# Two feed-forward stages: the up products over an operand whose high and low parts lie side by side

## The chip, the cores and the metric

The kernel runs on one core of one Trainium2 chip. The metric is device time in microseconds of one execution, as the median of several. One execution was also taken with the hardware profiler, and all rows below come from that one.

## The reference, cut to what matters

The program is a transformer layer for 256 tokens of 1024 features, all in float32: two attention kinds and a mixture of experts in a first block, then a second block of axial attention, cross attention, feed-forward 0, a mixer, cross attention, feed-forward 1 and a final norm. The change is about the two feed-forward stages:

```python
x = x + conv_gated_ffn(rmsnorm_2(x, ffn_norm[i]), ffn_w_up[i], ffn_conv_w[i],
                       ffn_conv_b[i], ffn_w_down[i])

# conv_gated_ffn: up to 2 x 2816 features, a convolution of three taps
# along the tokens with a bias, then
    return (jax.nn.silu(gate) * val) @ w_down
```

So each token's 1024 features are divided by their root mean square and multiplied by a gain, widened to 5632 features, mixed with the neighbour tokens' values, gated, and brought back to 1024 features.

## The kernel before, in words

**Numbers in two parts.** A float32 value is kept as a high part and a low part. A product of two such values is three matmuls, low by high, high by high and high by low, all added in PSUM (`mm3`, L363 to L366). The weights pass through in blocks of 128x1024: SP's queue loads a block (`w`), ACT copies its high part at L275 (`whi`, four buffers), DVE subtracts at L284 (`wlo`, three buffers), and PE uses the pair. `get` hands out block n and emits the high part of block n+3 and the low part of block n+2, so the `wlo` of block n+2 goes to the buffer that block n-1 leaves, and waits in DVE's order until PE is done with block n-1.

**A feed-forward stage** (`ffn`, L1751) has 22 steps j. In a step, `up(j)` (L1767) takes two blocks: for each, eight chunks of 128 rows, each with three matmuls of 256 columns (`two_blocks`, 48 matmuls, into one PSUM bank, tags "s" and "tp" by turns). Then `act_steps(j)` follows on DVE and ACT: `u` = sums times 1/rms (DVE, L1777), `y` = middle tap and bias (ACT, L1782, two of them), the two other taps (DVE, four of L1786/L1787), the gate (ACT, L1789), their product (DVE, L1791), its high part `gTh` (ACT, L1793) and its low part `gTl` (DVE, L1795). `down(j-3)` (L1802) is 12 matmuls of 512 columns with `gTh` and `gTl` as the stationary side, into four PSUM banks that collect over the whole stage. Its fifth matmul is the first that reads `gTl`.

The operand of `up` is x times gain, not yet divided by the rms: the stage begins while the last residual sums are still being added. The root comes behind it: `columns` three blocks in, `rows` (L467) four blocks in, and `nrep` (L473) then holds 1/rms along the free axis for L1777. Four `turn`s (L1809, at j = 4, 8, 12, 16) transpose the residual for the end of the stage.

**What sets the order.** Each engine runs its instructions in the order in which the program emits them. `act_steps` is a generator. After each weight block, `tick` lets the generators in `side` advance by turns until a credit is spent; `finish` advances them until the named one has ended, and `down_all(j)` calls it for step j before its matmuls. The blocks of a stage follow as: up(0) 0, 1; up(1) 2, 3; up(2) 4, 5; up(3) 6, 7; down(0) 8; up(4) 9, 10; down(1) 11; up(5) 12, 13; down(2) 14; and so on, three a step.

Of the kernel before, what the change touches and what calls it, by code (L numbers as in the profile page):

```python
# [32 lines left out]
T = 256  # L33
NT = 2
# [29 lines left out]
def _constants():  # L64
# [23 lines left out]
    # mean over the window of each group, minus the token itself  # L88
# [62 lines left out]
def body(tc, a, out, dbg=None):  # L151
# [44 lines left out]
    # keys and values of the memory, to be worked on wherever TensorE would wait  # L196
# [39 lines left out]
    with top:  # L236
# [8 lines left out]
        ps = pool(top, "ps", space=PS)  # L245
        NB = {"mm": 3, "s": 3, "tp": 2}

        def bank(tag="mm", dt=FT):
            return ps.tile([128, 512], dt, name=tag, tag=tag, bufs=NB[tag])

# [16 lines left out]
        def cuts(n, f):  # L267
            # the very first block in halves, to begin earlier
            return [slice(0, f // 2), slice(f // 2, f)] if n == 0 else [slice(0, f)]
# [89 lines left out]
        def split_to(hi, lo, src):  # L359
            S.activation(hi, src, AF.Copy)  # L360
            V.tensor_sub(lo, src, hi.bitcast(FT))

# [13 lines left out]
        # (the tables of ScalarE come in while the first loads run)  # L376
# [19 lines left out]
        class Norm:  # L396
# [21 lines left out]
            def square(self, p):  # L418
# [25 lines left out]
            def squares(self):  # L444
                """their squares over the head width, for the norms of the heads"""
# [15 lines left out]
            def spread(self):  # L461
                """1/rms of the tokens, along the free axis of every partition."""
# [15 lines left out]
        def h_pair():  # L478
            return (hp.tile([128, KC, T], FR, name="hTh", tag="hTh"), hp.tile([128, KC, T], FR, name="hTl", tag="hTl"))
# [11 lines left out]
        def two_blocks(aT, blocks, o, lead=False):  # L491
            """two blocks of 128 features; as a lead side by side, for an operand whose last chunks are still to come"""
# [16 lines left out]
        class Feat:  # L509
            """features on partitions: two blocks of 128 a bank"""  # L510
# [24 lines left out]
        class Tok:  # L535
            """tokens on partitions: 512 features, a bank for each half of the tokens"""
# [32 lines left out]
        def head_roots(stk, sq, H, nm, t):  # L569
            """1/rms of the heads, without that of the tokens"""  # L570
# [6 lines left out]
        def flip_heads(dst, src, t, two=False):  # L577
            """dst[feature, pair, token] from src[token, head, 64]; `two` doubles each head into a pair"""
# [98 lines left out]
            # what the scores of each head are scaled by: 1/rms, and 1/8  # L677
# [169 lines left out]
                # a block for each head of a pair  # L847
# [3 lines left out]
            # -- stages of causal attention for the two heads of a pair --  # L851
# [54 lines left out]
            # -- projections and the compressed keys and values --  # L906
# [64 lines left out]
            # -- the heads, pair by pair, with projections in between --  # L971
# [81 lines left out]
            # -- merge: g0 * up_a(ya) + g1 * up_b(yb), with g = (1 + tanh) / 2 --  # L1053
# [36 lines left out]
        # high and low parts of the keys side by side  # L1090
# [37 lines left out]
        # -- routing, a few operations at a time --  # L1128
# [17 lines left out]
        def route():  # L1146
# [12 lines left out]
            def keys(q):  # L1159
                """keys of the kept pairs, of four heads"""  # L1160
                hs, ks = ts(q, 4), ts(q, 64)
                for t in range(NT):
# [11 lines left out]
                    for e in range(2):  # L1174
# [3 lines left out]
                        if q == 0:  # L1178
                            # (whole numbers: 1 where they are equal, 0 elsewhere)
# [36 lines left out]
            # gates: softmax over the kept ones  # L1216
# [16 lines left out]
            # the gates (in 0..1, times GATE) as a sum of two float16 parts  # L1233
# [40 lines left out]
        # -- gates in place: one-hot products, two tokens side by side --  # L1274
# [22 lines left out]
        def one_hot(half, j):  # L1297
            # the wide scratch of the norms is free here
# [53 lines left out]
        # -- second products; their sum goes to the residual --  # L1352
# [643 lines left out]
```

## Time and profile before

| | us |
|---|---|
| three runs | 1767.97, 1765.30, 1765.14 |
| median | 1765.3 |
| span of the profiled execution | 1767.7 |
| PE busy in that span | 1734.9 (98%) |
| DVE busy | 1375.0 (78%) |
| ACT busy | 940.7 (53%) |

The profile's span is that of one execution of its own, 2.4 us above the median of the timed ones. Busy time of PE counts the whole of pipelined matmuls; the distance from one matmul's start to the next one's is what tells how fast they go. Feed-forward 0 lies from about 1256 to 1447 us of the span, feed-forward 1 from about 1569 us to the end.

### The profile page before, as it was taken

The numbers are of one execution on the slowest core, as the hardware profiler recorded it, in microseconds if no ns is written. First come the engines' busy times: TensorE is split into PE (matmuls) and PEld (weight loads), VectorE is DVE, ScalarE is ACT, GpSimd is POOL, SyncE is SP. The second block draws the span as 40 slices with busy tenths as digits, with TensorE's granted clock in tenths as the row PEclk, the third lists the DMA queues.
The fourth block names the chain that finished last, engine by engine and source line by source line (L and its number), as shares of the span: only waits on it lengthen the run. The fifth ranks groups of instructions, "written<-read, shape, count | busy, mean of one in ns | idle before, by whom it ended". The sixth has DMA issues, their size and how long they took to land. (4 is left out here: it accounts for less than half of the span.)

```text
span 1767.7 us, 32012 instructions
## 1 busy us (share of the span) xinstructions
PE 1734.9 (98%) x12638; PEld 1579.8 (89%) x12638; DVE 1375.0 (78%) x2435; ACT 940.7 (53%) x1396; POOL 174.7 (10%) x127
## 2 busy tenths in 40 slices
PE   8999999999999999999999999999999999999998
PEld 7877999999999998888888887799999999899997
DVE  7788879999878776999666657875788876678777
ACT  5556555455544344444454554655566566556555
POOL 1210020155200000000010003010200002020000
PEclk9999999999999999999999999999999999999999
DMA  6633454555544545555655654243556554455553
GB/s 210 202 121 100 148 166 161 195 168 168 193 164 167 166 161 186 164 173 167 214 190 191 194 170 153 84 156 121 192 181 202 179 174 160 132 183 189 179 181 129
DMA packets 83094, 297.66 MB, mean 168 GB/s; under 512 B 9264, under 2 KB 10304, under 8 KB 82816
## 3 DMA queue, kind: packets, MB, share of 16 engines
q1 hardware_dynamic: 81072, 291.41, 49.9%
q0 software_dynamic: 608, 2.62, 0.4%
q8 instruction: 99, 1.62, 0.4%
q10 hardware_dynamic: 1264, 1.59, 0.3%
q14 instruction: 51, 0.42, 0.1%
HBM read 294.54 MB, written 1.05 MB: 167 GB/s over the span
## 5 line engine op out<-in xcount | busy, mean ns | idle before, releaser
L275 ACT ACTIVATE whi<-w 128x1024 fp32r<-128x1024 f32 (+1 forms) x554 | 583.1, 1055 | 445.8 <-PE s L1366 151.8
L284 DVE TENSOR_TENSOR wlo<-w,whi 128x1024 fp32r<-128x1024 f32 (+1 forms) x554 | 700.2, 1269 | 148.2 <-issue 67.4
L364 PE MATMUL s<-hTl,whi 128*128 128x256 f32 x1024 | 292.5, 286 | 0.0
L366 PE MATMUL s<-hTh,wlo 128*128 128x256 f32 x1024 | 290.2, 283 | 1.2 <-DVE wlo L284 1.1
L365 PE MATMUL s<-hTh,whi 128*128 128x256 f32 x1024 | 289.6, 283 | 0.0
L366 PEld LDWEIGHTS s<-hTh,wlo 128*128 128x128 f32 x1024 | 196.3, 192 | 2.1 <-DVE wlo L284 2.0
L364 PEld LDWEIGHTS s<-hTl,whi 128*128 128x128 f32 x1024 | 196.3, 192 | 0.1
L365 PEld LDWEIGHTS s<-hTh,whi 128*128 128x128 f32 x1024 | 196.4, 192 | 0.0
L364 PE MATMUL mm<-hTl,whi 128*128 128x256 f32 (+1 forms) x488 | 140.1, 287 | 0.0
L366 PE MATMUL mm<-hTh,wlo 128*128 128x256 f32 (+1 forms) x488 | 138.8, 285 | 0.8 <-DVE wlo L284 0.7
L365 PE MATMUL mm<-hTh,whi 128*128 128x256 f32 (+1 forms) x488 | 138.7, 284 | 0.0
L1366 PE MATMUL mm<-wlo,hTh 128*128 128x512 f32 x381 | 131.3, 398 | 0.0
L1366 PE MATMUL mm<-whi,hTh 128*128 128x512 f32 x381 | 128.4, 390 | 0.0
L1366 PE MATMUL mm<-whi,hTl 128*128 128x512 f32 x381 | 128.1, 390 | 0.0
L364 PE MATMUL tp<-xTl,whi 128*128 128x256 f32 x352 | 99.7, 283 | 0.0
L366 PE MATMUL s<-xTh,wlo 128*128 128x256 f32 x352 | 99.6, 283 | 0.0
L366 PE MATMUL tp<-xTh,wlo 128*128 128x256 f32 x352 | 99.6, 283 | 0.0
L365 PE MATMUL s<-xTh,whi 128*128 128x256 f32 x352 | 99.5, 283 | 0.0
L365 PE MATMUL tp<-xTh,whi 128*128 128x256 f32 x352 | 99.4, 282 | 0.0
L364 PE MATMUL s<-xTl,whi 128*128 128x256 f32 x352 | 98.9, 281 | 0.0
L366 PEld LDWEIGHTS mm<-hTh,wlo 128*128 128x128 f32 (+1 forms) x488 | 93.6, 192 | 1.3 <-DVE wlo L284 1.2
L364 PEld LDWEIGHTS mm<-hTl,whi 128*128 128x128 f32 (+1 forms) x488 | 93.4, 191 | 0.7 <-issue 0.4
(451 smaller groups left out, 3914.4 us busy)
## 6 DMA issues: line engine op xcount, KB each, us to landing
w<-in_p_u_dram SPq DMA_DIRECT2D x128, 512.0 KB, 3.3
w<-in_p_v_dram SPq DMA_DIRECT2D x128, 512.0 KB, 3.3
w<-in_f_up_dram SPq DMA_DIRECT2D x88, 512.0 KB, 3.2
w<-in_f_down_dram SPq DMA_DIRECT2D x44, 512.0 KB, 3.8
w<-in_w_tok_dram SPq DMA_DIRECT2D x19, 512.0 KB, 3.4
w<-in_w_mg_dram SPq DMA_DIRECT2D x16, 512.0 KB, 3.5
w<-in_p_wq_dram SPq DMA_DIRECT2D x16, 512.0 KB, 3.3
w<-in_x_k_dram SPq DMA_DIRECT2D x16, 512.0 KB, 3.4
```

Source lines behind the costliest of these rows:

```text
L275: S.activation(hi[:, c], w[:, c], AF.Copy)
L284: V.tensor_sub(lo[:, c], w[:, c], hi[:, c].bitcast(FT))
L364: mm(o, l[0], r[1], start=start, stop=False, **kw)
L365: mm(o, l[0], r[0], start=False, stop=False, **kw)
L366: mm(o, l[1], r[0], start=False, stop=stop, **kw)
L1366: mm(acc[2 * h + t], l[k], w[m][:, ts(h, 512)], start=c == 0 and k == 0 and m == 1, stop=c == 127 and k == 1)
```

## The change

Up to the sixth step a stage runs as before, over x times gain. From the seventh on (`J0 = 6`) it runs over an operand that is already divided by the rms, `hN`.

- `h_pair` is now one tile with the high and the low part of each chunk next to each other (this holds for every user of `h_pair`).
- `normed_steps`, a generator among the others, makes `hN` once 1/rms is there: four DVE multiplications of 128x512, eight ACT copies and eight DVE subtractions of 128x256.
- `mm_side` takes the place of `mm3` in the steps from j = 6: for each chunk, the high weights run once over 512 columns (high and low part of `hN`), the low weights over 256. The two halves of the result stand in two halves of a bank.
- `act_steps` from j = 6: ACT copies the second half, DVE adds the first to it. This replaces the multiplication by 1/rms.
- PSUM: the banks are closed and opened anew for each stage. `up` gets two tiles of two banks each, the sums of `down` four banks that `columns`, `rows` and the turns use first. All four turns are now at j = 1 and 2. Before a tile is taken again, `wait_freed` advances the generators until its sums have been read.

```diff
         def h_pair():
-            return (hp.tile([128, KC, T], FR, name="hTh", tag="hTh"), hp.tile([128, KC, T], FR, name="hTl", tag="hTl"))
+            return Pair(hp.tile([128, KC, 2, T], FR, name="hT", tag="hT"))
...
+        def mm_side(o, w, aT):
+
+            for kc in range(KC):
+                mm(o, w[0][:, ts(kc)], merge(aT.t[:, kc]), start=kc == 0, stop=kc == KC - 1, skip_group_check=True)
+                mm(o[:, 0:T], w[1][:, ts(kc)], aT[0][:, kc], start=False, stop=kc == KC - 1, skip_group_check=True)
...
+                def normed_steps():
+
+                    for p in range(4):
+                        tag = ("nsq", "nacc")[p % 2]
+                        x = pairs(st_.tile([128, 512], FT, name=tag, tag=tag, bufs=1))
+                        V.tensor_tensor(x, xT[:, 2 * p:2 * p + 2], nm_.rep2(), op=OP.mult)
+                        yield
+                        for k in range(2):
+                            c = 2 * p + k
+                            g = gcol[:, gi, c:c + 1]
+                            S.activation(hN[0][:, c], x[:, k], AF.Copy, scale=g)
+                            V.scalar_tensor_tensor(hN[1][:, c], x[:, k], g, hN[0][:, c].bitcast(FT), op0=OP.mult, op1=OP.subtract)
+                        yield
+
+                J0 = 6
+                after(3, first_columns)
+                after(4, first_rows)
...
+                        o = Banks.pool.tile([128, 1024], FT, name="up", tag="up", bufs=2)
+                    if j < J0:
+                        if j % 2 == 0:
+                            first_up[0] = o
+                        o = first_up[0][:, ts(j % 2, 512)]
+                        two_blocks(hT, blocks, o, j == 0)
+                        tick()
+                        return o
+                    finish(normed)
+                    for e in range(2):
+                        mm_side(o[:, ts(e, 512)], get(*blocks[e]), hN)
+                        tick()
                     return o
...
-                    V.tensor_tensor(u, pairs(o), nm_.rep2(), op=OP.mult)
+                    if j < J0:
+                        V.tensor_tensor(u, pairs(o), nm_.rep2(), op=OP.mult)
+                    else:
+                        ov = o.rearrange("p (e s t) -> p e s t", e=2, s=2)
+                        S.activation(u, ov[:, :, 1], AF.Copy)
+                        yield
+                        V.tensor_tensor(u, ov[:, :, 0], u, op=OP.add)
+                    freed.add(j)
...
                 for j in range(NJ):
                     o = up(j)
+                    if j == 1 or j == 2:
+                        turn(2 * j - 2)
+                        turn(2 * j - 1)
+                    if j == 3:
+                        acc_[:] = [side_bank() for _ in range(4)]
                     acts.append(spawn(act_steps(j, o)))
```

On PE, a piece of one `up` in the steps from the seventh on. Before, three matmuls a chunk, with `xTl` and `xTh` as the low and high part of the operand:

```order
L364 MATMUL s<-xTl,whi 128x256
L365 MATMUL s<-xTh,whi 128x256
L366 MATMUL s<-xTh,wlo 128x256
L364 MATMUL s<-xTl,whi 128x256
L365 MATMUL s<-xTh,whi 128x256
L366 MATMUL s<-xTh,wlo 128x256
```

and now, with the end of the `down` before it, two a chunk:

```order
L1895 MATMUL acc<-wlo,gTh 128x512 x2
L1895 MATMUL acc<-whi,gTh 128x512 x2
L1895 MATMUL acc<-whi,gTl 128x512 x2
L388 MATMUL up<-hT,whi 128x512
L389 MATMUL up<-hT,wlo 128x256
L388 MATMUL up<-hT,whi 128x512
L389 MATMUL up<-hT,wlo 128x256
```

The columns of a chunk are the same, 768, in two matmuls and two weight loads where there were three of each.

On DVE, feed-forward 0, from the low weights of block 5 on. Before (y_14486/7 are the two halves of step 0, y_14557/8 of step 1), up to `gTl` of step 0:

```order
L1777 TENSOR_TENSOR u<-tp,nrep 128x512
L1786 SCALAR_TENSOR_TENSOR y_14486<-u,cw,y_14486 128x255
L1787 SCALAR_TENSOR_TENSOR y_14486<-u,cw,y_14486 128x255
L1786 SCALAR_TENSOR_TENSOR y_14487<-u,cw,y_14487 128x255
L1787 SCALAR_TENSOR_TENSOR y_14487<-u,cw,y_14487 128x255
L284 TENSOR_TENSOR wlo<-w,whi 128x1024 x2
L1786 SCALAR_TENSOR_TENSOR y_14557<-u,cw,y_14557 128x255
L1787 SCALAR_TENSOR_TENSOR y_14557<-u,cw,y_14557 128x255
L1786 SCALAR_TENSOR_TENSOR y_14558<-u,cw,y_14558 128x255
L1787 SCALAR_TENSOR_TENSOR y_14558<-u,cw,y_14558 128x255
L1791 TENSOR_TENSOR y_14486<-y_14486,y_14487 128x256
L284 TENSOR_TENSOR wlo<-w,whi 128x1024
```

Now (y_14529/30 are step 0), the piece around the product of step 0 and its `gTl`, with the low weights of blocks 9 and 10:

```order
L298 TENSOR_TENSOR wlo<-w,whi 128x1024
L1817 TENSOR_TENSOR nsq<-xT,nrep 128x512
L1884 TENSOR_TENSOR y_14529<-y_14529,y_14530 128x256
L1823 SCALAR_TENSOR_TENSOR hT<-nsq,first,hT 128x256 x2
L1888 TENSOR_TENSOR gTl<-y_14529,gTh 128x256
L298 TENSOR_TENSOR wlo<-w,whi 128x1024
L1434 SCALAR_TENSOR_TENSOR meml<-memT,first,memh 128x256
L1864 TENSOR_TENSOR u<-up,nrep 128x512
```

and the rows behind it, where y_14716/7 are the halves of step 1 and y_14761/2 those of step 2, and the two low weights are those of blocks 11 and 12:

```order
L1817 TENSOR_TENSOR nacc<-xT,nrep 128x512
L298 TENSOR_TENSOR wlo<-w,whi 128x1024
L1823 SCALAR_TENSOR_TENSOR hT<-nacc,first,hT 128x256 x2
L298 TENSOR_TENSOR wlo<-w,whi 128x1024
L1879 SCALAR_TENSOR_TENSOR y_14716<-u,cw,y_14716 128x255
L1880 SCALAR_TENSOR_TENSOR y_14716<-u,cw,y_14716 128x255
L1879 SCALAR_TENSOR_TENSOR y_14717<-u,cw,y_14717 128x255
L1880 SCALAR_TENSOR_TENSOR y_14717<-u,cw,y_14717 128x255
L1864 TENSOR_TENSOR u<-up,nrep 128x512
L1884 TENSOR_TENSOR y_14716<-y_14716,y_14717 128x256
```

What moved: the taps of step 1 stood ahead of step 0's product and of the low weights of block 9; now they stand behind the low weights of block 12, and the rows that make `hN` (L1817, L1823) are in between. Feed-forward 1 has the same order there.

## Rows read from the trace of the kernel before

**Rows 1.** The page: span, and each engine's busy time, share and instructions.

```profile
span 1767.7 us, 32012 instructions
PE 1734.9 (98%) x12638; PEld 1579.8 (89%) x12638; DVE 1375.0 (78%) x2435; ACT 940.7 (53%) x1396; POOL 174.7 (10%) x127
```

**Rows 2.** Steps of feed-forward 0 as one stretch; PEclk is the granted clock.

```profile
core 0: us, PE busy (x) PEld busy (x) DVE busy (x) ACT busy (x) POOL busy (x), PEclk, DMA share, GB/s
1282.00:1440.00 158.00, 158.00 (x1107) 147.59 (x1106) 131.02 (x202) 98.55 (x148) 1.07 (x2) 1.00 0.56 186
```

**Rows 3.** PE timeline, one step of feed-forward 0: start, duration, instruction.

```profile
1333.89 0.63 PE L1802 MATMUL mm<-wlo,gTh 128*128 128x512 f32 x2
...
1336.46 0.39 PE L1802 MATMUL s<-whi,gTl 128*128 128x512 f32 x1
1336.69 0.28 PE L364 MATMUL s<-xTl,whi 128*128 128x256 f32 x1
...
1342.45 0.64 PE L1802 MATMUL mm<-wlo,gTh 128*128 128x512 f32 x2
...
1350.89 0.29 PE L366 MATMUL tp<-xTh,wlo 128*128 128x256 f32 x1
1351.02 0.64 PE L1802 MATMUL mm<-wlo,gTh 128*128 128x512 f32 x2
```

**Rows 4.** PE timeline, the experts' second products: first and last of a stretch.

```profile
860.00 0.62 PE L1366 MATMUL mm<-wlo,hTh 128*128 128x512 f32 x2
...
870.88 0.62 PE L1366 MATMUL mm<-wlo,hTh 128*128 128x512 f32 x2
```

**Rows 5.** Timelines of PE and DVE where the feed-forward stages begin.

```profile
1569.17 0.28 PE L364 MATMUL s<-xTl,whi 128*128 128x256 f32 x1
...
1569.37 0.69 DVE L560 TENSOR_TENSOR xT<-xT,mm 128x512 f32<-128x512 f32 x1 [0.24 <-PE mm L366]
...
1269.61 0.68 PE L467 MATMUL tp<-ndg,ones 128*128 128x128 f32 x4 [1.05 <-DVE ndg L458]
```

**Rows 6.** Durations of the normalised operand made elsewhere (tile hn): min/median/max ns.

```profile
L1123 ACT ACTIVATE hTh<-hn,first x8: 493/496/499, 286.7 to 289.5; 128x256 fp32r<-128x256 f32 x8
L1124 DVE SCALAR_TENSOR_TENSOR hTl<-hn,first,hTh x8: 465/476/477, 288.1 to 290.8; 128x256 fp32r<-128x256 f32 x8
```

**Rows 7.** A stretch of feed-forward 1's first steps, columns as in rows 2.

```profile
1582.00:1594.00 12.00, 12.00 (x98) 11.86 (x98) 11.25 (x18) 9.22 (x15) 0.00 (x0) 1.00 0.49 165
```

**Rows 8.** DVE timeline of feed-forward 1, steps 0 and 1.

```profile
1584.24 0.68 DVE L1777 TENSOR_TENSOR u<-tp,nrep 128x512 f32<-128x512 f32 x1
1584.84 0.47 DVE L1786 SCALAR_TENSOR_TENSOR y<-u,cw,y 128x255 f32<-128x255 f32 x1
...
1586.66 2.35 DVE L284 TENSOR_TENSOR wlo<-w,whi 128x1024 fp32r<-128x1024 f32 x2
1588.93 0.48 DVE L1786 SCALAR_TENSOR_TENSOR y<-u,cw,y 128x255 f32<-128x255 f32 x1
...
1590.76 0.42 DVE L1791 TENSOR_TENSOR y<-y,y 128x256 f32<-128x256 f32 x1
1591.10 1.22 DVE L284 TENSOR_TENSOR wlo<-w,whi 128x1024 fp32r<-128x1024 f32 x1
```

**Rows 9.** ACT timeline of feed-forward 1: the y pair, and gTh of step 0.

```profile
1583.22 1.09 ACT L1782 ACTIVATE y<-u,cw 128x256 f32<-128x256 f32 x2 [0.76 <-DVE u L1777]
...
1591.21 0.42 ACT L1793 ACTIVATE gTh<-y 128x256 fp32r<-128x256 f32 x1 [1.33 <-DVE y L1791]
```

**Rows 10.** A long PE wait and the clock behind it, then a short one.

```profile
1068.30 1.02 PE L434 MATMUL tp<-ones,nacc 128*128 128x2 f32 x4 [2.90 <-POOL nacc L428]
...
1068.00:1072.00 4.00, 3.70 (x11) 3.12 (x12) 1.63 (x4) 1.06 (x1) 0.96 (x2) 0.50 0.35 131
1072.00:1076.00 4.00, 4.00 (x14) 3.15 (x13) 1.35 (x5) 2.07 (x5) 0.00 (x0) 0.66 0.40 131
1268.00:1272.00 4.00, 2.95 (x25) 2.77 (x24) 2.12 (x4) 0.91 (x3) 2.12 (x3) 1.00 0.65 219
```

More of the change, by code (lines that the diff above doesn't have):

```diff
@@ L244, in body, with open, close @@
         hp = pool(top, "h")
-        ps = pool(top, "ps", space=PS)
         NB = {"mm": 3, "s": 3, "tp": 2}
+        class Banks:
+            stack = pool = None
+            @classmethod
+            def open(cls, name):
+                cls.stack = ExitStack()
+                cls.pool = pool(cls.stack, name, space=PS)
+            @classmethod
+            def close(cls):
+                cls.stack.close()
+        Banks.open("ps")
         def bank(tag="mm", dt=FT):
-            return ps.tile([128, 512], dt, name=tag, tag=tag, bufs=NB[tag])
+            return Banks.pool.tile([128, 512], dt, name=tag, tag=tag, bufs=NB[tag])
         class Stream:
@@ L361, in split_to, with __new__ @@
             V.tensor_sub(lo, src, hi.bitcast(FT))
+        class Pair(tuple):
+            def __new__(cls, t):
+                self = tuple.__new__(cls, (t[:, :, 0], t[:, :, 1]))
+                self.t = t
+                return self
+        def mm_side(o, w, aT):
+            for kc in range(KC):
+                mm(o, w[0][:, ts(kc)], merge(aT.t[:, kc]), start=kc == 0, stop=kc == KC - 1, skip_group_check=True)
+                mm(o[:, 0:T], w[1][:, ts(kc)], aT[0][:, kc], start=False, stop=kc == KC - 1, skip_group_check=True)
         def mm3(o, l, r, start, stop, **kw):
@@ L1358, in w_split @@
             h, cc = divmod(c, HALF)
-            split_to(*(merge(x) for x in cut(wT, ALL, slice(c % 8, c % 8 + 2))), merge(A[h][:, cc:cc + 2]))
+            split_to(*cut(wT, ALL, slice(c % 8, c % 8 + 2)), A[h][:, cc:cc + 2])
         def v_mm(c, w, t, hs=(0, 1)):
@@ L1715, in fin @@
                             mm3(o[:, ts(c, T)], cut(xv[i], ALL, k, ts(cc)), cut(pT, ALL, k), k == 0, k == 1)
-                    split_to(merge(oT[0][:, 2 * h:2 * h + 2]), merge(oT[1][:, 2 * h:2 * h + 2]), o)
+                    split_to(oT[0][:, 2 * h:2 * h + 2], oT[1][:, 2 * h:2 * h + 2], pairs(o))
                 ss = [sco(0), sco(1)]
@@ L1758, in ffn @@
                 nc.sync.dma_start(cw, a[f"f_conv{i}"])
-                acc_ = [bank("mm") for _ in range(3)] + [bank("s")]
-                acc[:] = acc_
                 nm_ = nm
-                after(3, nm_.columns)
-                after(4, nm_.rows)
+                gi = nm_.gi
                 gTs = {}
-                tags = ["s", "tp"]
-                def up(j):
-                    o = bank(tags[j % 2])
-                    two_blocks(hT, [(f"f_up{i}", e * NJ + j) for e in range(2)], o, j == 0)
-                    tick()
+                acc_ = []
@@ new lines, in ffn, with side_bank, first_columns, first_rows @@
+                hN = h_pair()
+                def side_bank():
+                    return Banks.pool.tile([128, 512], FT, name="acc", tag="acc", bufs=4)
+                def first_columns():
+                    o = side_bank()
+                    for t in range(NT):
+                        mm(o[:, 2 * t:2 * t + 2], nm_.acc[:, ts(t)], ones[:, 0:2], start=True, stop=True)
+                    nm_.root(o)
+                def first_rows():
+                    nm_.diagonal()
+                    o = side_bank()
+                    for t in range(NT):
+                        mm(o[:, ts(t)], ones, nm_.dg[:, t], start=True, stop=True)
+                    nm_.rep = st_.tile([128, T], FT, name="nrep", tag="nrep", bufs=1)
+                    S.activation(nm_.rep, o[:, 0:T], AF.Copy)
+                    normed.append(spawn(normed_steps()))
@@ new lines, in ffn, with wait_freed @@
+                normed = []
+                J0 = 6
+                after(3, first_columns)
+                after(4, first_rows)
+                first_up, freed = [None], set()
+                def wait_freed(ks):
+                    while not freed.issuperset(ks):
+                        step()
+                def up(j):
+                    blocks = [(f"f_up{i}", e * NJ + j) for e in range(2)]
+                    if j >= J0 or j % 2 == 0:
+                        if j >= J0 + 2:
+                            wait_freed([j - 2])
+                        elif j >= J0:
+                            wait_freed([2 * j - J0 - 4, 2 * j - J0 - 3])
+                        elif j >= 4:
+                            wait_freed([j - 4, j - 3])
+                        o = Banks.pool.tile([128, 1024], FT, name="up", tag="up", bufs=2)
[10 more added lines that the diff above has]
+                        tick()
@@ L1803, in down, with turn @@
                                stop=j == NJ - 1 and k == 1)
-                def turn(j, p):
-                    o = bank(tags[j % 2])
+                def turn(p):
+                    o = side_bank()
                     for t in range(NT):
@@ L1812, in ffn @@
                 finish()
+                Banks.close()
+                Banks.open(f"pf{i}")
                 pace[0] = 2 * STEP
@@ L1830, in ffn @@
                         finish()
-                    if j >= 4 and j % 4 == 0 and j // 4 <= 4:
-                        turn(j, j // 4 - 1)
                 down_all(NJ - 3)
@@ L1844, in ffn @@
                         done(t, h, st)
+                Banks.close()
+                Banks.open(f"ps{i}")
                 tick()
@@ L1975, in body @@
         ffn(1, xk_, last)
+        Banks.close()
         fs.close()
```

## The prediction

> **What bounds the kernel now.** I read the page's busy line first: PE is busy for 1734.9 of 1767.7 us, DVE for 1375.0, ACT for 940.7 [rows 1]. PE's instructions set the time, and the question is only where PE would wait instead. Next the stage itself: over 158 us of feed-forward 0 PE is busy without a break at a granted clock of 1.00 (2.4 GHz), DVE for 131.02 us (83%), ACT for 98.55 us (62%) [rows 2]. So DVE has 17% of the stage left, and there is no PE wait in it that the change could remove. A gain can come from shorter matmul work alone, and a loss from DVE or ACT being late.
>
> Then one step, matmul by matmul [rows 3]. A step runs from 1333.89 to 1342.45, 8.56 us. Its 12 matmuls of 512 columns take 1336.69 - 1333.89 = 2.80, that is 0.2333 each; its 48 of 256 columns take 5.76, that is 0.120 each.
>
> **The shorter matmul work.** A chunk of up is three matmuls now, 3 x 0.120 = 0.360 us. It becomes one of 512 columns and one of 256. The columns are equal in sum, so what is saved is what a matmul costs beyond its columns, once a chunk. This is small here, since the 512-column slot (0.2333) is nearly twice the 256-column one: 0.2333 + 0.120 = 0.3533, a saving of 0.0067. The new pattern alternates widths, which before happens only at the two crossings of a step: 512 before 256 is 0.23 apart (1336.46 to 1336.69), 256 before 512 is 0.13 apart (1350.89 to 1351.02) [rows 3]; their sum 0.36 would save nothing. The other end is the 512-column slot where DVE is less busy, 48 of them from 860.00 to 870.88, 0.2267 each [rows 4]: 0.3467 and a saving of 0.0133. From the seventh to the last step there are 16 steps x 2 blocks x 8 chunks in each of two stages, 512 chunks. So the gain lies between 0 and 6.8 us. I take 0.354 a chunk, close to the stage's own averaged slots and a little towards the crossings: 0.006 x 512 = **3.1 us**.
>
> A 512-column matmul takes 0.2333 here and a 256-column one 0.120 [rows 3]. The Trainium skill, page "TensorE: Matmul & The Clock Gate", section "Back-to-back issue gap", gives an isolated gap of N/2.4 + 2.5 ns at the full clock, and this speaks against the change: only 2.5 ns a chunk would be saved, an estimate of 1.3 us in all, and the end would be 1773.1. The same section has a sustained figure of 131 ns for 512 columns, by which the change would be worth far more; the slots of 0.2267 to 0.2333 [rows 3, 4] bear that out nowhere.
>
> **The start of a stage.** The first up matmul of feed-forward 1 stands at 1569.17, before the last residual add has even begun (DVE L560 at 1569.37, 0.69 long, which reads the sums of the last cross-attention pair) [rows 5]. In the changed kernel the banks are closed and opened anew; the first up tile takes banks in which those sums stand, so the matmul waits for the add: 1569.37 + 0.69 + about 0.1 is 1570.2, **1.0 us** later. In feed-forward 0 it is the same size, but there PE waits 1.05 us for the root before 1269.61 [rows 5], and that wait hangs on DVE and POOL, not on PE; it swallows the delay. Cost 0 there.
>
> **What steps 1 to 5 now carry.** Making hN adds on DVE four multiplications (0.60 apart, as the u's of the same shape at 1584.24 to 1584.84 [rows 8]) and eight subtractions of 0.476 [rows 6], 6.2 us a stage, and on ACT eight copies of 0.496 [rows 6], 4.0 us. DVE has no room for it just there: from 1582 to 1594 us it is busy for 11.25 of 12.00 us [rows 7]. Moving all turns to j = 1 and 2 adds no transposes; their four ACT evacuations come earlier, where ACT has 9.22 of 12 us [rows 7].
>
> The order shows where the time is taken from. Before, the taps of step 1 ran at 1588.93, before step 0's product at 1590.76 [rows 8]. Now they stand behind the low weights of block 12, and these wait until PE is done with block 9, the first block of up(4). Call that moment t0. From t0 PE has the second block of up(4), 24 x 0.120 = 2.88 us; then it wants down(1), which needs gTh of step 1. On the path, with spacings of the DVE timeline [rows 8]: DVE's release 0.24 [rows 5], low weights 1.13 (half of the 2.27 from 1586.66 to 1588.93), four taps 1.82 (1584.84 to 1586.66), u of step 2 0.68: 3.9. ACT has the two y's of step 2 ahead of gTh, 1.09, then gTh 0.42 [rows 9]: **5.4**. PE waits 5.4 - 2.88 = 2.5 us. gTl of step 1 stands behind the four taps of step 2, which begin when the first y is there at about 4.45 and end at 6.3, so it is ready at 6.8; the fifth matmul of down(1) wants it at 5.4 + 4 x 0.2333 = 6.3: 0.5 more. **3.0 us a stage, 6.0 in both.**
>
> down(0) in the same way, from t1, the end of up(3)'s first block, for which the low weights of block 9 wait. DVE: 0.24 + 1.13, x 0.60, product 0.42, at 2.4; gTh at 2.8, just before PE's 2.88. But ACT then makes two copies of hN (2 x 0.49, to 3.8), DVE their second subtraction (to 4.3), and gTl behind it is ready at 4.7, wanted at 2.88 + 0.93 = 3.8: 0.9 us, **1.8 in both**. In feed-forward 0, up(4) finds its tile held by u of step 1, which stands behind gTl of step 0, low weights 1.13, one subtraction for the memory 0.48 and its own 0.68: 6.9 after t1, wanted at 2.88 + 2.80 + 0.9 = 6.6: **0.3**.
>
> From down(2) on the same path leaves some tenths of a microsecond, and from the seventh step each step's u has a step's time. There ACT's copy of 512 values a partition, about 0.6 a step, lies in its 38% of free time [rows 2], and the DVE add takes the place of a multiplication of the same shape. The new layout of hT elsewhere, and closing and opening banks at a stage's end, I cost at nothing: the same instructions over the same number of values.
>
> **Sum.** Against the profiled execution's 1767.7: -3.1 + 1.0 + 6.0 + 1.8 + 0.3 = +6.0, so 1773.7 in a profile. The median of the runs before is 2.4 lower, 1765.3, and so the forecast is **1771.3**. Bounds: with the gain at its ends 1767.6 and 1774.4.
>
> **The rivals.**
> Rival 1, the clock falls as well. A PE wait of 2.90 us is followed by a granted clock of 0.50 and 0.66 (1.2 GHz for most of it) in the next two stretches of 4 us [rows 10]; that is 3.70 x 0.50 = 1.9 and 4.00 x 0.34 = 1.4 us of lost work. After the wait of 1.05 us the clock stays at 1.00 [rows 10]. down(1)'s wait of 2.5 us, with 0.9 some 6 us ahead, is nearer to the long one. If it falls in both stages, 1.9 to 3.2 us each come on top: 1775.1 to 1777.7, say 1776.4. Against it: the wait is shorter than the one seen, and up to it PE was busy throughout.
>
> Rival 2, no change that can be told. Either the gain is at its upper end with the waits as worked out, 1767.6, or the waits are half as long because DVE arrives at those places less laden than I assume, 1765.3 + 4.5 - 3.1 = 1766.7. For it: each wait is the difference of two chains of some 5 us, so a tenth of error in a few operations matters. Against it: the order puts step 1's taps behind t0 whatever their durations.
>
> Rival 3, faster. The gain is 6.8, as in [rows 4], and the waits shrink to the start's 1.0 and about 1.0 in all: 1760.5. It needs both; the slots of [rows 3], from the very stage, speak against the first, and [rows 7] against the second. It decides from the point where the waits are under the gain.
>
> **How the numbers follow.** Forecast 0.45, its own range 1769 to 1774.4; rival 1 0.21; rival 2 0.20; rival 3 0.14. About 0.2% (3.5 us) is what a measurement of this kernel can tell from no change. The forecast is at +0.34%, and rival 1 beyond it: slower 0.64. Of the forecast's 0.45 some 0.02 lie under 1768.8 and so within the bound: same 0.20 + 0.02 = 0.22. Faster 0.14. The range leaves out rival 3 for the most part and rival 1's far end: 1762.5 to 1777.0.
>
> **What would show it.** In the profile after: PE's slots in up from the seventh step, 512 before 256 at about 0.233 and 256 before 512 at about 0.12 (a step of 8.46 instead of 8.56); were the 512 slot 0.2267 there, the gain is the upper one. A wait of about 2.5 us on PE before down(1) in each stage, for gTh or ACT, and a smaller one in down(0) for gTl; none there means the loss is not what I think. A first up matmul of feed-forward 1 some 1.0 after the last cross-attention matmul. The granted clock in the 8 us after down(1)'s wait tells rival 1 from the forecast. What would make the prediction wrong: waits in every step from the seventh on, for a tile of up or for ACT's copy; or a slot of 256 columns behind one of 512 that isn't 0.12.

## The result and the profile after

| | before | after |
|---|---|---|
| median of the timed runs (4 each) | 1765.82 us | 1783.36 us (1780.56 to 1786.07) |
| ratio | | 1.0096, 95% interval 1.0084 to 1.0108 |
| span of the profiled execution | 1767.7 us | 1780.5 us |

The kernel became slower by 17.5 us; the forecast was 6.0 slower, and its range ended at 1777. In the page's busy line, which answers to [rows 1], PE hardly differs in share, although it issues 512 matmuls fewer:

```profile
span 1780.5 us, 31131 instructions
PE 1736.1 (98%) x12126; PEld 1552.8 (87%) x12126; DVE 1386.9 (78%) x2459; ACT 958.5 (54%) x1444; POOL 173.0 (10%) x127
```

So one has to look into the two stages. PE's waits from 1240 us on (engine, line, what it waited for: us in all, times, longest) are new ones; before, that list held 1.0 us for the root and 0.8 us besides:

```profile
PE acc L1895 <- ACT gTh L1886: 9.0, 5, 2.8
PE acc L1895 <- DVE gTl L1888: 2.9, 6, 0.8
PE up L392 <- DVE xT L588: 1.7, 2, 0.9
```

All of it is down waiting for gTh and gTl, and the first up of a stage waiting for the last sums of x. From the last matmul of the cross attention to the last of down, feed-forward 0 took 192.21 us before and 198.81 after (1253.56 to 1452.37), feed-forward 1 190.98 and 199.98: 15.6 more in both. The spans of these two executions are only 12.8 apart, because the one of before reached feed-forward 0 2.8 us later (1256.32 against 1253.56): before it had the 2.90 us wait and the slow clock of [rows 10], and the one of after waited only 1.61 us at that place and kept its clock. That is in no line that the change touches.

**The gain.** One step of up after (start, duration, instruction; answers to [rows 3]), and the first matmuls of down(3) and down(17) in feed-forward 1:

```profile
1338.33 0.40 PE L388 MATMUL up<-hT,whi 128*128 128x512 f32 x1
1338.56 0.28 PE L389 MATMUL up<-hT,wlo 128*128 128x256 f32 x1
1338.68 0.39 PE L388 MATMUL up<-hT,whi 128*128 128x512 f32 x1
...
1630.92 0.63 PE L1895 MATMUL acc<-wlo,gTh 128*128 128x512 f32 x2
...
1748.43 0.63 PE L1895 MATMUL acc<-wlo,gTh 128*128 128x512 f32 x2
```

A chunk takes 0.35 (0.23 and 0.12), and the 14 steps from down(3) to down(17) take 117.51, 8.39 each; before, a step was 8.57. That is 0.17 us a step, 5.5 us in 32 steps.

**down(0).** PE and DVE in feed-forward 0:

```profile
1281.00 0.63 PE L1895 MATMUL acc<-whi,gTh 128*128 128x512 f32 x2
1282.09 0.73 PE L1895 MATMUL acc<-whi,gTl 128*128 128x512 f32 x2 [0.46 <-DVE gTl L1888]
...
1283.48 0.68 DVE L1864 TENSOR_TENSOR u<-up,nrep 128x512 f32<-128x512 f32 x1
1284.22 0.39 PE L392 MATMUL up<-xTl,whi 128*128 128x256 f32 x1
```

gTl holds the fifth matmul for 0.6 us. The first matmul of up(4) comes at 1284.22, just behind the u of step 1 that frees its tile and 0.2 later than at full pace.

**down(1).** The chain in feed-forward 0, as the prediction followed it:

```profile
1287.59 1.22 DVE L298 TENSOR_TENSOR wlo<-w,whi 128x1024 fp32r<-128x1024 f32 x1
1288.72 0.48 DVE L1879 SCALAR_TENSOR_TENSOR y<-u,cw,y 128x255 f32<-128x255 f32 x1
...
1290.55 0.68 DVE L1864 TENSOR_TENSOR u<-up,nrep 128x512 f32<-128x512 f32 x1
...
1291.27 1.09 ACT L1875 ACTIVATE y<-u,cw 128x256 f32<-128x256 f32 x2 [1.04 <-DVE u L1864]
1292.27 0.40 ACT L1886 ACTIVATE gTh<-y 128x256 fp32r<-128x256 f32 x1
...
1292.72 0.74 PE L1895 MATMUL acc<-wlo,gTh 128*128 128x512 f32 x2 [2.48 <-ACT gTh L1886]
```

The low weights of block 12 begin behind up(4)'s first block, step 1's taps behind them, then u of step 2, its two y on ACT, and gTh of step 1. PE's last matmul before stood at 1289.96: with its own 0.12 taken off, 2.64 us are lost.

Just before, DVE stood idle. Three times in feed-forward 0 a subtraction of hN waits for the ACT copy that it reads, 2.8 us in all (the third 0.89 is at 1286.78):

```profile
1276.91 0.88 DVE L1823 SCALAR_TENSOR_TENSOR hT<-nacc,first,hT 128x256 fp32r<-128x256 f32 x2 [0.98 <-ACT hT L1822]
1280.81 0.89 DVE L1823 SCALAR_TENSOR_TENSOR hT<-nsq,first,hT 128x256 fp32r<-128x256 f32 x2 [0.89 <-ACT hT L1822]
```

**The tail.** Behind the last up four downs follow, 18 to 21. They begin at 1436.25. Before, they begin at 1437.53. PE after, within them:

```profile
1436.25 0.62 PE L1895 MATMUL acc<-wlo,gTh 128*128 128x512 f32 x2
...
1444.20 0.49 PE L1895 MATMUL acc<-wlo,gTh 128*128 128x512 f32 x1 [1.73 <-ACT gTh L1886]
...
1445.69 0.80 PE L1895 MATMUL acc<-whi,gTl 128*128 128x512 f32 x1 [0.77 <-DVE gTl L1888]
...
1447.07 0.63 PE L1895 MATMUL acc<-whi,gTh 128*128 128x512 f32 x1
1447.49 0.63 PE L1895 MATMUL acc<-whi,gTl 128*128 128x512 f32 x1
...
1452.60 0.28 PE L392 MATMUL mm<-meml,whi 128*128 128x256 f32 x1
```

From 1436.25 to 1452.60 it is 16.35 us; before, 11.23 (1437.53 to 1448.76). Two things are seen: waits for gTh and gTl, and matmuls of 512 columns 0.42 apart instead of 0.233. DVE shows why gTh is late. These are the u of steps 20 and 21, before and after:

```profile
1430.31 0.68 DVE L1777 TENSOR_TENSOR u<-s,nrep 128x512 f32<-128x512 f32 x1
1438.88 0.68 DVE L1777 TENSOR_TENSOR u<-tp,nrep 128x512 f32<-128x512 f32 x1
```

```profile
1434.88 0.68 DVE L1869 TENSOR_TENSOR u<-up,u 128x512 f32<-128x512 f32 x1
1442.04 0.68 DVE L1869 TENSOR_TENSOR u<-up,u 128x512 f32<-128x512 f32 x1
```

Before, u of step 20 runs 7.2 us ahead of the last four downs (1437.53) and u of step 21 1.4 us behind their start. After, u of step 20 runs only 1.4 us ahead of them (1436.25) and u of step 21 5.8 us behind. Each step's work comes some 5 us later than before, and in the tail there is no further up to cover that.

This lateness stands from the seventh step on. In feed-forward 1 down(3) begins at 1630.92 and down(17) at 1748.43 (above); the u of steps 6 and 20 come 7.0 us behind these:

```profile
1637.90 0.68 DVE L1869 TENSOR_TENSOR u<-up,u 128x512 f32<-128x512 f32 x1
...
1755.40 0.68 DVE L1869 TENSOR_TENSOR u<-up,u 128x512 f32<-128x512 f32 x1
```

Before, the same distance is 2.2 us at step 6 and 1.4 at step 20. So the delay from the first steps is carried through the whole stage.

**The clock.** Stretches of the profile after, columns as in [rows 2]:

```profile
1446.00:1449.00 3.00, 3.00 (x7) 2.06 (x7) 2.25 (x3) 1.48 (x3) 0.00 (x0) 0.50 0.00 0
1612.00:1617.00 5.00, 4.90 (x15) 3.47 (x16) 4.48 (x8) 1.33 (x4) 0.00 (x0) 0.66 0.26 77
```

The granted clock is 0.50 (1.2 GHz) in the tail of feed-forward 0 behind waits of 1.73 and 0.77, and falls in down(1) of feed-forward 1 behind a wait of 2.75; behind the 2.48 of feed-forward 0 it stayed at 1.00.

### The profile page after: what moved, and what is told of

It is laid out like the page before. It is cut to its first block, busy times and chain, and to the rows that moved or that the text cites. A ratio compares the mean times of both kernels' runs of the same rounds, so it can differ in the third digit from the quotient of the medians.

```text
span 1780.5 us, 31131 instructions
## 1 busy us (share of the span) xinstructions
PE 1736.1 (98%) x12126; PEld 1552.8 (87%) x12126; DVE 1386.9 (78%) x2459; ACT 958.5 (54%) x1444; POOL 173.0 (10%) x127
## 5 line engine op out<-in xcount | busy, mean ns | idle before, releaser
L394 PE MATMUL s<-hT,wlo 128*128 128x256 f32 x1024 | 290.4, 284 | 2.4 <-DVE wlo L298 2.2
L392 PE MATMUL s<-hT,whi 128*128 128x256 f32 x1024 | 292.5, 286 | 0.0
L393 PE MATMUL s<-hT,whi 128*128 128x256 f32 x1024 | 289.6, 283 | 0.0
L1394 PE MATMUL mm<-whi,hT 128*128 128x512 f32 x762 | 235.3, 390 | 0.0
L394 PEld LDWEIGHTS s<-hT,wlo 128*128 128x128 f32 x1024 | 196.2, 192 | 3.5 <-DVE wlo L298 3.4
L392 PEld LDWEIGHTS s<-hT,whi 128*128 128x128 f32 x1024 | 196.3, 192 | 0.1
L393 PEld LDWEIGHTS s<-hT,whi 128*128 128x128 f32 x1024 | 196.4, 192 | 0.0
L388 PE MATMUL up<-hT,whi 128*128 128x512 f32 x512 | 180.5, 395 | 0.0
L1394 PEld LDWEIGHTS mm<-whi,hT 128*128 128x128 f32 x762 | 143.0, 188 | 30.7
L389 PE MATMUL up<-hT,wlo 128*128 128x256 f32 x512 | 143.5, 280 | 0.0
L392 PE MATMUL mm<-hT,whi 128*128 128x256 f32 (+1 forms) x488 | 139.4, 286 | 0.0
L393 PE MATMUL mm<-hT,whi 128*128 128x256 f32 (+1 forms) x488 | 137.9, 283 | 0.0
L392 PEld LDWEIGHTS mm<-hT,whi 128*128 128x128 f32 (+1 forms) x488 | 92.7, 190 | 0.7 <-issue 0.4
L393 PEld LDWEIGHTS mm<-hT,whi 128*128 128x128 f32 (+1 forms) x488 | 92.8, 190 | 0.3
```

Source lines behind the costliest of these rows:

```text
L388: mm(o, w[0][:, ts(kc)], merge(aT.t[:, kc]), start=kc == 0, stop=kc == KC - 1, skip_group_check=True)
L389: mm(o[:, 0:T], w[1][:, ts(kc)], aT[0][:, kc], start=False, stop=kc == KC - 1, skip_group_check=True)
L392: mm(o, l[0], r[1], start=start, stop=False, **kw)
L393: mm(o, l[0], r[0], start=False, stop=False, **kw)
L394: mm(o, l[1], r[0], start=False, stop=stop, **kw)
L1394: mm(acc[2 * h + t], l[k], w[m][:, ts(h, 512)], start=c == 0 and k == 0 and m == 1, stop=c == 127 and k == 1)
```

## The experiments

### The tail: the last steps hastened

```diff
                 for j in range(NJ):
+                    pace[0] = (3 if j >= 16 else 2) * STEP
                     o = up(j)
```

> The changed kernel, but from step 16 on three steps of act_steps may follow each weight block instead of two, so that the last steps' taps, products and gT are emitted right behind their up. Theory (the order at the end of a stage: the work of steps 19 to 21 is emitted late, PE waits for gTh and gTl there and the clock falls behind it): each stage's tail loses its 5.1 us of extra time, 10.2 in all, so about 1773. Rival (ACT's copy and the longer chain of the new steps are the cost, whatever their order): at most 1 to 2 us a stage are saved, 1779 to 1782.

Measured: 1772.26 us, 11.1 below the changed kernel's first median; ratio to before 1.0029 (1.0017 to 1.0042). The waits of the tail are gone; u of steps 20 and 21 stand at 1430.71 and 1439.07, 6.7 us ahead of the last four downs and 1.7 behind their start, nearly as before the change. PE from the first matmul of the last two downs to the last one:

```profile
1443.00 0.39 PE L1895 MATMUL acc<-wlo,gTh 128*128 128x512 f32 x1
...
1443.76 0.50 PE L1895 MATMUL acc<-wlo,gTh 128*128 128x512 f32 x1
...
1448.53 0.39 PE L1895 MATMUL acc<-whi,gTl 128*128 128x512 f32 x1
```

5.53 us from the first start to the last, 23 slots of 0.24. So the 10 us of the two tails were the place of the last steps in the order, not the longer chain of a step; the rival falls.

### The clock: useless matmuls in the waits

```diff
+                    if j == 1:
+                        idle_mm(first_up[0][:, 512:1024], w, 10)
...
+                idle_mm(ups[NJ - 2][:, 0:512], ws[0], 7)
```

> The changed kernel with matmuls of no use put where PE waits: ten of 512 columns ahead of down(1), seven ahead of the last two downs, into bank halves that nothing reads. They are extra work, 2.3 and 1.6 us, shorter than the waits. Theory (behind the long waits the clock falls, and that is part of the loss): PE's slots stay at 0.233 behind these places, 1.2 us in down(1) of feed-forward 1 and 1.5 in each tail are saved, about 1779. Rival (the clock has no part in it): 1783 as without them, or up to 2 more where the extra matmuls outlast the wait.

> The changed kernel itself once more, beside the others of this call: 1780 to 1786 as before.

Measured side by side: 1779.34 us with them, 1785.20 without, 1.0078 (1.0060 to 1.0096) and 1.0107 (1.0090 to 1.0124) of before. More work, and some 6 us less time. PE in feed-forward 0 with the extra matmuls, and the clock there:

```profile
1290.98 2.44 PE L1838 MATMUL up<-whi 128*128 128x512 f32 x10
1293.63 0.74 PE L1901 MATMUL acc<-wlo,gTh 128*128 128x512 f32 x2 [0.21 <-ACT gTh L1892]
...
1444.00:1449.00 5.00, 3.85 (x15) 2.24 (x14) 4.16 (x9) 2.84 (x6) 0.00 (x0) 1.00 0.01 4
```

Nothing that PE waits for comes sooner, but the clock stays at 1.00 and the matmuls behind are 0.233 apart. In the profile of the repeated changed kernel, the granted clock fell at all four places (down(1) and tail of both stages, 0.72 to 0.76 in the 5 to 7 us around each), in the first profile at three. So about a third of the loss (5.9 of 19.6 us) is the clock behind the waits. The length of a wait does not decide alone: behind the 2.48 us of feed-forward 0 the clock stayed in the first profile and fell in the repeated one, and behind 2.74 in feed-forward 1 it stayed at 1.00 in the run with the hastened tail. That may be a part of the spread of these runs; no run shows it.

### down(0) and down(1): without hN

```diff
-                    normed.append(spawn(normed_steps()))
-                J0 = 6
+                J0 = NJ
```

> The changed kernel with J0 = 22: no step runs over the normalised operand, hN is not made; the new banks, the layout of hT, the moved turns and the start remain. Theory (the waits of down(0), down(1) and of the tail all come from making and using hN): only the 1.0 us at the start of feed-forward 1 is left, 1766 to 1768. Rival (the banks, the four early turns and the order of PSUM use cost by themselves): waits before down(0) and down(1) remain, 1770 or more.

Measured: 1770.43 us, 1.0028 (1.0016 to 1.0039). down(0) to down(1) takes 8.56, as before, so the waits there belong to hN, to its work or to its turns. The number lies in the rival's range, but not for the rival's reason: 2.9 us of PE waits remain that neither theory had, in second blocks of up:

```profile
1292.58 0.69 DVE L1863 TENSOR_TENSOR u<-up,nrep 128x512 f32<-128x512 f32 x1 [0.76 <-PE up L394]
...
1293.42 0.36 PE L392 MATMUL up<-xTl,whi 128*128 128x256 f32 x1 [0.88 <-DVE u L1863]
```

In the steps before J0, here all of them, two steps share one tile of two banks. u of the even step, emitted between the two blocks of the odd one, reads the first bank; the second block waits for it although it writes the other bank. The price is that of sharing a tile, 0.9 at the first place.

### down(0) and down(1): place in the order, or time on DVE

Steps that take their turn and do nothing (the steps from the seventh on use x times gain):

```diff
                     for p in range(4):
...
-                        V.tensor_tensor(x, xT[:, 2 * p:2 * p + 2], nm_.rep2(), op=OP.mult)
                         yield
-                        for k in range(2):
...
                         yield
...
-                        mm_side(o[:, ts(e, 512)], get(*blocks[e]), hN)
+                        mm_side(o[:, ts(e, 512)], get(*blocks[e]), hT)
```

> The changed kernel, but the eight steps that make hN do nothing, though they still take their turns and their credit; the steps from the seventh on run over the operand x times gain instead (laid side by side too), so that their results lack the division by the rms. Step 1's taps stand behind the low weights of block 12 as before. Theory (place in the order): down(1) still waits 2.5 to 2.8 us for gTh and the tail stays; only down(0)'s 0.9 a stage goes, about 1781. Rival (time on DVE): the waits of down(0) and down(1) go, 1783 to 1785 - 8 to 10, about 1775.

Measured: 1784.84 us, 1.0101 (1.0081 to 1.0120). PE at down(1), feed-forward 0:

```profile
1291.99 0.89 PE L1885 MATMUL acc<-wlo,gTh 128*128 128x512 f32 x2 [2.36 <-ACT gTh L1876]
```

The wait is there with no work of hN on DVE at all; down(0)'s is gone. It is nearly 4 us more than expected: the clock fell behind down(1) in both stages (0.72 in the 6 us around each), it was low for longer in the two tails (0.51 and 0.52 over 7 us; each tail takes 1.1 more than in the changed kernel's first profile), and the steps take 8.44 instead of 8.39. The turns that the generator of hN takes are enough to make down(1)'s wait. They are enough for the tail too: u of the later steps comes 7.0 us behind the down as with hN, and both tails wait 1.73 and 0.76.

hN made as in the change, but step 1 emitted ahead of up(4), with the tail mended:

```diff
+                    if j == 4:
+                        finish(acts[1:2])
                     o = up(j)
```

> The changed kernel with hN made as in it, but all steps of step 1 are emitted ahead of up(4), ahead of the low weights of blocks 11 and 12, and the last steps are hastened as in the first run of this study. Theory (place in the order): down(1)'s wait goes and nothing takes its place, 1772 - 6 to 8, 1765 to 1767. Rival (time on DVE): the low weights of blocks 11 and 12 are late instead, or down(0) waits longer; 1769 or more.

Measured: 1779.85 us, 1.0081 (1.0064 to 1.0098), 7.6 more than with the tail mended alone. PE in feed-forward 0:

```profile
1292.68 0.70 PE L1895 MATMUL acc<-wlo,gTh 128*128 128x512 f32 x2 [3.02 <-DVE wlo L298]
...
1298.65 0.55 PE L392 MATMUL up<-xTl,whi 128*128 128x256 f32 x1 [2.92 <-DVE u L1864]
```

gTh is in time, and now down(1)'s low weights are late, and u behind them. That looks like the rival, but the run does not separate the two: `finish` advances the generators by turns, so the taps of step 2 (1289.14 to 1290.98) now stand ahead of these low weights too, and DVE again stood idle for 2.8 us because subtractions of hN waited for ACT's copies. That DVE has no time for hN is thus not shown; moving the subtractions further behind the copies was not tried. Three steps behind each block through the whole stage:

```diff
-                pace[0] = 2 * STEP
+                pace[0] = 3 * STEP
```

> The changed kernel with three steps behind each weight block instead of two through the whole of a feed-forward stage. Step 1's taps then stand behind the low weights of block 10 instead of 12, and the tail is as in the run in which only the last steps were hastened. Theory (the place of the instructions in DVE's order makes the waits, not their sum): the waits of down(1) and those of the tail go, 1764 to 1767. Rival (DVE has no room for the 6.2 us of making hN in steps 1 to 5, whatever the order): waits of 2 us and more a stage stay or move to other steps, 1769 to 1772.

Measured: 1777.11 us, 1.0054 (1.0038 to 1.0071): the tail is mended, and in feed-forward 0 PE waits 0.5 and 1.6 for step 1's gTh and gTl and 2.7 for u. The waits moved, as the rival says, but the time lies above its range too. Spreading hN's work over six steps:

```diff
-                J0 = 6
+                J0 = 10
...
+                    if 4 <= j < J0:
+                        next(normed[0], None)
+                        next(normed[0], None)
```

> The changed kernel, but hN is made from step 4 to step 9, two of its twelve pieces behind each down, outside the credit of the other steps, and J0 = 10. Theory (hN's instructions ahead of step 1's taps make the waits of down(0) and down(1)): these waits, 0.9 and 3.4 a stage with 1.2 of a slow clock in feed-forward 1, go; four steps a stage lose 0.17 us each of gain. 1783.4 - 9.8 + 1.3, so about 1775, with the tail as before. Rival (these waits come from the early turns or the banks): they stay, about 1785.

Measured: 1776.52 us, 1.0054 (1.0037 to 1.0071), near the 1775 expected, but not for the reason given. down(0) to down(1) is 8.56 again; in its place feed-forward 0 waits 3.2 for u and 2.1 for hN (feed-forward 1: 1.7 and 1.0), and the tail of feed-forward 1 lost its waits, which was not meant. Here hN takes no turn among the other steps, and u of steps 9 to 20 in feed-forward 1 comes 1.7 to 3.1 us behind the down instead of 7.0. This fits the run of empty turns: the tail's waits come from a delay that the turns make at the start.

hN on POOL, with the tail mended:

> hN made by POOL instead of DVE (multiplications by 1/rms and gain, subtractions; the copies stay on ACT), outside the credit of the other steps, and the last steps hastened as in the first run of this study; J0 = 6. Theory (DVE has no room for hN in steps 1 to 5; the order alone does not help): the waits of down(0) and down(1) go, up(4) waits some 0.9 for u of step 1; 1772.3 - 8.0 + 2.0, about 1766, and with the gain of 5.4 it is level with the kernel before. Rival (DVE's load is not it, or POOL's work slows DVE): waits of 2 us and more remain, 1769 or more.

```diff
-                        V.tensor_tensor(x, xT[:, 2 * p:2 * p + 2], nm_.rep2(), op=OP.mult)
+                    G.tensor_tensor(x, xT[:, 2 * p:2 * p + 2], nm_.rep2(), op=OP.mult)
...
+                        G.tensor_tensor(hN[1][:, c], xs[p][:, k], hN[0][:, c].bitcast(FT), op=OP.subtract)
```

Measured: 1776.02 us, 1.0056 (1.0039 to 1.0073), the rival's side. The waits of down(0) and down(1) are gone, and one of 4.5 stands in up(5). DVE, POOL and PE in feed-forward 0:

```profile
1288.12 0.84 DVE L1885 SCALAR_TENSOR_TENSOR y<-u,cw,y 128x255 f32<-128x255 f32 x1
1288.89 1.51 DVE L1884 SCALAR_TENSOR_TENSOR y<-u,cw,y 128x255 f32<-128x255 f32 x1
...
1288.77 1.35 POOL L1818 TENSOR_TENSOR nsq<-xT,nrep 128x512 f32<-128x512 f32 x1
...
1301.29 0.55 PE L392 MATMUL up<-xTl,whi 128*128 128x256 f32 x1 [4.49 <-DVE u L1869]
```

While POOL works, DVE's eight taps from 1287 to 1298 us take 0.71 to 1.51 us where they take 0.48. POOL is no free engine for this work.

### The banks at the start

```diff
                 Banks.open(f"pf{i}")
+                side_bank()
```

> The changed kernel with one more tile of the collecting banks taken ahead of all others, so that up's tiles and the collecting banks lie the other way round and up(0) no longer meets the last sums of the cross attention. Theory (the first up waits for the bank): the wait of 0.87 us before the first up matmul goes in both stages; in feed-forward 0 the wait for the root grows by about as much, in feed-forward 1 1.0 us is saved. Rival (it waits for the add because of the tile of x itself): the wait stays.

Measured once: 1783.80 us (span 1781.6). The wait before the first up is gone in both stages, and the root's wait is back at 0.75 in feed-forward 0, as the theory says. But the collecting banks now lie where the next stage begins:

```profile
1454.42 0.39 PE L392 MATMUL mm<-meml,whi 128*128 128x256 f32 x1 [0.81 <-DVE xtok L1940]
```

0.8 us come back there; the total says nothing at this size.

### No normalised operand

x times gain, laid side by side, serves the later steps as well; DVE adds and then multiplies:

```diff
-                        mm_side(o[:, ts(e, 512)], get(*blocks[e]), hN)
+                        mm_side(o[:, ts(e, 512)], get(*blocks[e]), hT)
...
                         V.tensor_tensor(u, ov[:, :, 0], u, op=OP.add)
+                        V.tensor_tensor(u, u, nm_.rep2(), op=OP.mult)
```

> No normalised operand: the operand x times gain of the first steps lies side by side, the steps from the fifth on (J0 = 4) run one matmul of 512 and one of 256 columns a chunk over it, ACT copies the second half, DVE adds and then multiplies by 1/rms; three steps behind each block. Theory (the matmul work saves 0.168 us a step, and all that the change lost lay in hN and in the order): 18 x 0.168 x 2 = 6.0 saved, 1.0 lost at the start of feed-forward 1, about 1760 to 1763. Rival (DVE at 83% cannot take 0.6 us more in each step): PE waits in most steps, 1767 or more.

Measured: 1768.45 us, 1.0012 (1.0002 to 1.0021), no gain. DVE's extra 0.6 us brought no wait in most steps, so the rival's reason fails too. But a step is 8.44, not 8.39; a second block of up waits 0.88 for u in the shared tile in each stage; and gTh is late by 1.2 and 0.6 in the tails.

> As the version without the normalised operand, but from the third step on (J0 = 2). Theory: two more steps a stage at 0.168 us, 0.7 less than with J0 = 4. Rival: up(3) has to wait for u of step 1, which needs 1/rms, and the gain is lost: 0 to 2 more than with J0 = 4.

Measured: 1767.47 us, 1.0004 (0.9995 to 1.0012). The shared tile's wait is gone; the tail of feed-forward 0 waits 2.2, longer than the 1.2 with J0 = 4:

```profile
1440.07 0.50 PE L1879 MATMUL acc<-wlo,gTh 128*128 128x512 f32 x1 [2.19 <-ACT gTh L1870]
```

How little the order helps by itself is seen in the kernel without the switch, with three steps behind each block:

> The kernel without the switch (J0 = 22) and with three steps behind each block. Theory (the 3 us that it lost beyond the start were waits of up for a tile whose u was emitted late): they go, 1766 to 1768. Rival (banks and early turns cost by themselves): 1770 as with two steps.

Measured: 1780.13 us, 1.0074 (1.0057 to 1.0091), 9.7 more than with two steps. u comes earlier in the order, more often between the two blocks of the step that shares its tile, and PE waits for it six times, 7.2 us in all and up to 2.4. Both theories fall.

With the two places mended (old form in the last two steps, the banks the other way round in feed-forward 1 alone):

```diff
+                    if j >= NJ - 2:
+                        o = o[:, 0:512]
+                        two_blocks(hT, blocks, o)
+                        tick()
+                        return o
...
+                if i == 1:
+                    side_bank()
```

> The version without the normalised operand and J0 = 2, with two places mended: the last two steps run in the old form (three matmuls a chunk, multiplication by 1/rms straight from PSUM), so that gTh of the last step comes sooner, and in feed-forward 1 alone the banks lie the other way round. Theory: the waits of 2.2 and 0.6 us in the two tails and the start's 1.0 in feed-forward 1 go, 0.5 of gain is given back; about 3 us less than that version's 1767.5, 1763 to 1765. Rival (what it saves in matmuls is taken by DVE's extra multiplication elsewhere): no change against it, 1766 to 1768.

Measured: 1762.18 us against 1765.60, 0.9981 (0.9971 to 0.9992), the only version here below the kernel before. PE's waits in both feed-forward stages:

```profile
PE acc L1884 <- ACT gTh L1875: 0.9, 2, 0.7
PE up L392 <- DVE xT L588: 0.9, 1, 0.9
```

## Why the prediction was wrong

The direction was right, the size was not: 17.5 us instead of 6.0. By its own terms, both stages, from the profile after:

| term | predicted | measured | from |
|---|---|---|---|
| shorter matmul work | -3.1 | -5.5 | 32 steps of 8.39 instead of 8.57 |
| start, feed-forward 1 | +1.0 | +1.0 | first up 1.16 behind the last cross-attention matmul |
| down(0) | +1.8 | +1.6 | 3.61 (3.78 less the 0.17 of the tile) and 3.62 instead of 2.80 |
| down(1) | +6.0 | +8.1 | 3.3 and 4.8; of the latter 1.2 are slower matmuls |
| tile of up(4), feed-forward 0 | +0.3 | +0.2 | first up(4) matmul 0.17 late |
| tail | 0 | +10.2 | 16.35 instead of 11.23; as much in feed-forward 1 |
| sum | +6.0 | +15.6 | as the two stages by themselves |

The step that failed is the sentence "from the seventh step each step's u has a step's time", by which the prediction put the end of the stage at nothing; it measured 10.2 us. It is true of the steps in the middle, where 3 steps of distance between up and down cover a late u, and it was not followed to the end of the stage, where the last up is followed by four downs alone. The prediction saw that step 1 is pushed back in DVE's order and charged down(1) for it, but took the delay as over by down(2); it stays at 7.0 us up to step 20. By the kernel's text this can be read: a step of the new form has six pieces that cost credit where the old one has five, and the three weight blocks of a step pay for six, so nothing is left to catch up with. That reading is an argument; the run with three pieces a block from step 16 on, which mends the tail, agrees with it. With this term alone the sum would have been 1781.5.

The chains of down(0) and down(1) were right to some tenths: down(0)'s gTl holds PE for 0.6 where 0.9 was worked out, down(1)'s gTh for 2.6 and 2.9 where it was 2.5. That feed-forward 0 absorbs the start's delay was right as well: the root's wait is not in the list of waits after.

The gain was mis-sized, within its bounds. The chunk takes 0.350, between the 0.3467 of the less laden stretch [rows 4] and the 0.3533 of the stage's own slots; the crossing of widths cost nothing more. By the isolated gap formula of the Trainium skill (page "TensorE: Matmul & The Clock Gate", section "Back-to-back issue gap") 1.3 us were to be saved, and 5.5 were: each chunk saved 11 ns where that formula gives 2.5. The sustained 131 ns for 512 columns of the same section are seen nowhere here: the slot stayed at 0.23 us.

Rival 1 (the clock) had a chance of 0.21 and was a part of what happened, on top of the forecast, at more places than it named. It priced a fall at 1.9 to 3.2 us; with useless matmuls in the waits 5.9 us are saved at four places, about 1.5 each.

What stays open: at down(1) the run of empty turns shows that the place in the order is enough to make PE wait (2.36 of 2.48 us). Whether DVE's time for hN would be enough by itself is not shown, since in the run with step 1 ahead of up(4) the order changed as well and DVE stood idle for ACT's copies. Why a step is 8.44 with x times gain and 8.39 with hN is open too. DVE's load is not the reason: in the run of empty turns, with the operand x times gain and no second multiplication, DVE is busy for 79.87 of 100 us in feed-forward 1 (1640 to 1740), against 80.01 in the changed kernel, and a step takes 8.44.

## What to carry to other kernels

When a change gives each step a longer chain or another turn in an emitted order, follow the chain at both ends of the loop: in the middle the distance between the loop's stages hides it, and the last iteration has nothing behind it. A short wait can cost more than its length, since the matmuls behind it may run at half the clock; look at their spacing, not at the wait alone. And where a saving in matmuls is bought with work on another engine, first ask whether that work is needed at all: the version that gained left the normalised operand out.

## What the runs showed of the hardware

A tap of 128x255 on DVE took 0.48 us, and 0.71 to 1.51 us while POOL ran multiplications and subtractions from SBUF. The Trainium skill (page "SBUF — State Buffer", section "SBUF: two separate sides") says that DVE and GpSimd share a pair of ports that one of them holds for a whole instruction; the rows agree: the tap beside a POOL instruction of 1.35 us takes 1.0 longer.

The granted clock fell to 0.50 behind waits of 1.73 and 0.77 us close together, and behind 2.36 in both stages of one run. Behind 2.48 at the same place of the same kernel it stayed at 1.00 in one execution and fell in another. Extra matmuls in the waits kept it at 1.00, and the kernel with more work was 5.9 us faster.
